# One decoder block on one core: attention steps in pairs, with the scores of four tiles in a row and one copy for two tiles

## The chip, the cores and the metric

The kernel runs on one core of one Trainium2 chip. The metric is the device time of one execution in microseconds (us). Of the engines, TensorE (PE in the profile; its weight loads are PEld), VectorE (DVE), ScalarE (ACT) and GpSimd (POOL) compute, and SyncE (SP) issues transfers. Each takes its instructions in the order in which they are written, and one engine waits for another through semaphores.

## The reference

One layer of a decoder block on an input of 1024 tokens by 1024 channels in float32. Two gated feed-forward half-steps stand around a middle part, which merges an attention and a pooling branch:

```python
h = h + 0.5 * swiglu(rms_norm(h, ffn1_norm), w1, w3, w2)
u = rms_norm(h, mix_norm);  q, k, v, pz, gates = split(u @ w_in)
y_attn = dilated_mixture_attention(q, k, v) @ w_branch_attn
y_pool = multiscale_pool(pz, pool_w, pool_scale) @ w_branch_pool
h = h + (sigmoid(gA) * y_attn + sigmoid(gB) * y_pool) @ w_out
h = h + 0.5 * swiglu(rms_norm(h, ffn2_norm), w1', w3', w2')
return rms_norm(h, final_norm)
```

The attention has 12 heads of 64 channels in three groups of four. A group has a window and a dilation: (128, 1), (512, 4), (2048, 16). A query attends to the keys t, t-r, t-2r and so on back to the window. The outputs of the three groups are added with weights from their softmax denominators.

## The kernel before

All products are made in single-precision parts: each operand is split into a high part and the rest, and three products (high by high, high by low, low by high) are added up in PSUM. The feed-forward halves and the input projection come first and last; they fill most of the time and the change does not touch them.

The change is in the attention loop (from line 1815). Its unit is a tile: one pair of heads (`hp`, two of them), one group (`g`, three) and one block of 128 queries (`i`, eight), which makes 48 tiles, listed in `slots`. A step `q` of the loop, 24 in all, takes the tiles 2q and 2q+1. Four steps make one pair of heads of one group. The order of the groups is 0, 1, 2 for the first pair of heads and 1, 2, 0 for the second. A tile has one or two blocks of keys (`blocks`): two in group 0 but for its first tile, one and two by turns in group 1, one in group 2.

The work of a tile runs through four steps of the loop, each engine in a written order (`manual_schedule`):

- `scores` (L1556): 6 matmuls a tile, three products for each of the two heads. The two heads use the lower and the upper 64 rows of the array, and each head writes a PSUM bank of its own. Banks come from two sets of four: "mm" for scores and rows of factors, "acc" for transposes, values and branch products. One bank is 512 columns of float32.
- `masked` (L1574): VectorE adds the mask and takes the row minimum; ACT makes the exponents (`exponents`, L1583).
- one step later `trans_p` (L1603): transposes of the exponents, which ACT splits (`ehi`, L1615) and VectorE completes (`elo`, L1618).
- two steps later `values` (L1636): the products with the values, both tiles of the step in one "acc" bank. 
- three steps later `gather` (L1654): VectorE copies them to `own`, 64 partitions by 128 elements, two copies a tile. In group 0 the 128 targets are next to each other, in group 1 they are 4 elements apart, in group 2 they are 8 apart.

Two things are woven in. `fill` (L1706) is the product of the pooling branch, which needs nothing of the attention: each `next(fill)` is four matmuls of 512 columns, three of them make one bank, and `end_branches` (L1720) multiplies that bank by the gate on VectorE. In the steps 18 to 21 the factors of the first pair of heads are applied: `f.rows()` transposes the factors of one group into an "mm" bank (L1537, four transposes, tile `fa`), and `f.product()` multiplies the gathered values by them on VectorE (L1673), which gives the bank back. Steps 18 and 20 make two such products each, 19 and 21 one each.

Beside that, ACT and GpSimd split the queries and keys of the next group (`split_ring`, L1216 and L1217), and SyncE loads what comes next.

Of the kernel before, what the change touches and what calls it, by code (L numbers as in the profile page):

```python
# [16 lines left out]
P = 128  # L17
S = 1024
D = 1024
NT = S // P  # L20
# [5 lines left out]
HD = 64  # L26
SC = HD ** -0.5
GROUPS = 3
# [8 lines left out]
def tokens(g, i):  # L37

    if g == 0:
        return i * P, 1, (i - 1 if i > 0 else None)  # L40
    if g == 1:
        r, b = divmod(i, 2)
        return r + 4 * P * b, 4, (i - 1 if b else None)
    return i, 8, None
# [74 lines left out]
def three(hi_lo_l, hi_lo_r):  # L119

    lh, ll = hi_lo_l
    rh, rl = hi_lo_r
    return ((lh, rh), (lh, rl), (ll, rh))
# [3 lines left out]
def tile_block(  # L127
# [29 lines left out]
    ve, ac, gp, pe = nc.vector, nc.scalar, nc.gpsimd, nc.tensor  # L157
# [10 lines left out]
    def bank(tag, name):  # L168
        return psum.tile([P, HALF], F32, tag=tag, name=name)
# [1032 lines left out]
    ring = {}  # L1202

    def load_ring(u, tile):

        ring[u] = []
        for a in range(2):
            y, hi = tile(F32, f"qk{u}_{a}_in"), tile(F32R, f"qk{u}_{a}_hi")
            nc.sync.dma_start(y, qk_dram[u][a].rearrange("h d c -> (h d) c"))
            ring[u].append((hi, y.bitcast(F32R), y))  # L1210

    def split_ring(u, n):

        hi, lo, y = ring[u][n // 2]
        c = (LOWS, HIGHS)[n % 2]
        ac.activation(hi[:, c], y[:, c], AF.Copy)  # L1216
        gp.tensor_tensor(lo[:, c], y[:, c], hi[:, c].bitcast(F32), op=OP.subtract)  # L1217
# [24 lines left out]
    def load_branch(d):  # L1242
        w, gb = row_part(f"wab{d}"), row(f"gb{d}")
        nc.sync.dma_start(w.rearrange("p (q c) -> p q c", q=2).bitcast(F32), late_w[1 + d][:, :, 256:768])
        nc.sync.dma_start(gb, gate_dram[d][:, 1])
        pool_in[d] = (w.rearrange("p (q c) -> p q c", q=2), gb)
# [116 lines left out]
    with tc.manual_schedule():  # L1363
# [4 lines left out]
        for k in range(len(items) + 4):  # L1368
# [6 lines left out]
            if k < len(items):  # L1375
                q, m = items[k]
# [3 lines left out]
            if k - 1 in results:  # L1380
                q, m = items[k - 1]
# [88 lines left out]
    slots = [(hp, g, i) for hp in range(HPAIRS) for g in ((0, 1, 2), (1, 2, 0))[hp] for i in range(NT)]  # L1470
    N = len(slots)
# [68 lines left out]
    def blocks(g, i):  # L1540

        return 1 if tokens(g, i)[2] is None else 2

    T = {}

    def scores(s):
        hp, g, i = slots[s]
        u = hp * GROUPS + g
        n = blocks(g, i)
        ks = slice((i + 1 - n) * P, (i + 1) * P)  # L1550
        ps = [bank("mm", f"s{s}_{a}")[:, :n * P] for a in range(2)]
        (qhi, qlo, _), (khi, klo, _) = ring[u]
        for j, (l, r) in enumerate(three((qhi, qlo), (khi, klo))):
            for a in range(2):
                rows = slice(a * HD, (a + 1) * HD)
                pe.matmul(ps[a], l[rows, i * P:(i + 1) * P], r[rows, ks], start=(j == 0), stop=(j == 2))  # L1556
        T[s] = {"s": ps}

    def masked(s):
        hp, g, i = slots[s]  # L1560
# [27 lines left out]
    def pair(q):  # L1588

        ns = [2 * blocks(*slots[s][1:]) * P for s in (2 * q, 2 * q + 1)]  # L1590
        return ((2 * q, 0, ns[0]), (2 * q + 1, ns[0], ns[1])), sum(ns)
# [16 lines left out]
    def split_p(q):  # L1608

        tiles, n = pair(q)  # L1610
        hi = a2.tile([P, 2 * HALF], F32R, tag="ehi", name=f"ehi{q}")
        lo = a2.tile([P, 2 * HALF], F32R, tag="elo", name=f"elo{q}")
        todo = tp.pop(q)
        for p, c0, w in todo:
            ac.activation(hi[:, c0:c0 + w], p, AF.Copy)  # L1615
        yield
        for p, c0, w in todo:
            ve.tensor_tensor(lo[:, c0:c0 + w], p, hi[:, c0:c0 + w].bitcast(F32), op=OP.subtract)  # L1618
        for s, c0, w in tiles:
            T[s]["pt"] = tuple(t[:, c0:c0 + w].rearrange("p (a b c) -> p a b c", a=2, c=P) for t in (hi, lo))  # L1620
        yield

    def values(q):
        both = bank("acc", f"o{q}")
        for s in (2 * q, 2 * q + 1):
            hp, g, i = slots[s]
            d = T[s]
            n = blocks(g, i)

            p = both[:, s % 2 * 2 * P:(s % 2 + 1) * 2 * P].rearrange("p (a c) -> p a c", a=2)  # L1630
            pt = d.pop("pt")
            j, end = 0, 3 * n - 1
            for b in range(n):
                c = slice((i + 1 - n + b) * P, (i + 2 - n + b) * P)
                for l, r in three(tuple(v[:, c] for v in v_of[hp * GROUPS + g]), tuple(w[:, :, b, :] for w in pt)):
                    pe.matmul(p, l, r, start=(j == 0), stop=(j == end))  # L1636
                    j += 1
            d["o"] = p
            if i == NT - 1:
                del v_of[hp * GROUPS + g]  # L1640

    own = {}

    def gather(s):

        hp, g, i = slots[s]
        p = T.pop(s)["o"]
        t0, step, _ = tokens(g, i)
        cols = slice(t0, t0 + step * (P - 1) + 1, step)
        if i == 0:  # L1650
            own[hp, g] = sums_o.tile([P, S], F32, tag="o", bufs=HPAIRS * GROUPS, name=f"o{hp}_{g}")
        for a in range(2):
            r = slice(a * HD, (a + 1) * HD)
            ve.tensor_copy(own[hp, g][r, cols], p[r, a, :])  # L1654

    att_parts = {}

# [69 lines left out]
    def send():  # L1727
        while stores:
            nc.sync.dma_start(*stores.pop())

    def branches():
        for n in range(2 * KT):
            yield from branch(n)

    fill = branches()
# [45 lines left out]
    def advance(gen, n=1):  # L1781
        for _ in range(n):
            next(gen, None)
# [24 lines left out]
    with tc.manual_schedule():  # L1808
        load_ring(uses[1], ring_tile)
        load_branch(1)  # L1810
        factors = [make_factors(hp, eng) for hp, eng in enumerate((gp, ve))]
        combines = [[Combine(hp, half, adds, lower) for half in range(2)]
                    for hp, (adds, lower) in enumerate((((gp, gp), gp), ((gp, ve), ve)))]
        splits = {}
        for q in range(N // 2):
            send()
            u, i = divmod(q, NT // 2)
            if 0 < u < len(uses) - 1 and i == 0:
                load_ring(uses[u + 1], ring_tile)
            scores(2 * q)  # L1820
            scores(2 * q + 1)
            if q == 1:
                next(fill)
                next(fill)
            if q > 0:
                trans_p(q - 1)
                splits[q - 1] = split_p(q - 1)
            if q > 1:
                next(fill, None)
                if q % 4 != 3:  # L1830
                    next(fill, None)
            if q > 2:
                gather(2 * q - 6)
                gather(2 * q - 5)
            masked(2 * q)
            masked(2 * q + 1)

            j = q - N // 4 - 6
            fa = [combines[0][j // 2]] * (2 - j % 2) if 0 <= j < 4 else []
            for f in fa:  # L1840
                f.rows()
            if q > 1:
                values(q - 2)
            if q > 0:
                advance(splits[q - 1], 2)
            for n in ((), (0,) if u > 0 else (), (2, 1) if u > 0 else (0, 2), (3,) if u > 0 else (1, 3))[i]:
                if u + 1 < len(uses):
                    split_ring(uses[u + 1], n)
            for f in fa:
                f.product()  # L1850
            end_branches()
            exponents(2 * q)
            exponents(2 * q + 1)
            house(2 * q)
            house(2 * q + 1)
        send()
        right_b.close()
        load_ya(3)
        load_merge(0)
        load_merge(1)  # L1860
        open_w_o()
        q = N // 2
        trans_p(q - 1)
        splits[q - 1] = split_p(q - 1)
        advance(factors[1])
        next(fill, None)
        values(q - 2)
        gather(2 * q - 6)
        gather(2 * q - 5)
        advance(splits[q - 1], 2)  # L1870
        advance(factors[1], 2)
        next(fill, None)
        end_branches()
        values(q - 1)
        for s in range(2 * q - 4, 2 * q):
            gather(s)
        for n in range(8):
            combines[1][n // 4].step()
            if n != 3:
                next(fill, None)  # L1880
            end_branches()
            send()
            if n == 3:
                load_merge(2)
        for k in (3, 4):
            load_merge(k)
# [34 lines left out]
    ops, banks = {}, {}  # L1921
# [66 lines left out]
    with tc.manual_schedule():  # L1988
# [66 lines left out]
        r = [rows_first2(t) for t in range(2)]  # L2055
# [211 lines left out]
```

## Time and profile before

| | |
|---|---|
| median of 3 runs | 1908.06 us (1907.91 to 1908.44) |
| the profiled execution: device time | 1908.0 us |
| its span, first to last instruction | 1906.2 us |
| granted TensorE clock | 0.999 |
| PE busy over the span | 1895.5 us (99%) |
| DVE, ACT, POOL busy over the span | 1336.2, 760.1, 731.0 us |
| the attention loop and its end | about 1042 to 1159 us of the span |

The profile is one execution. A line of a timeline gives start, duration, engine, source line and operation, output and inputs, shapes and count; lines of one kind that follow each other are merged. Starts of matmuls are recorded, their ends are modelled, so what counts on TensorE is the distance from one start to the next. The chain of waits is followed back from the last instruction and gives what was on the path at each time.

### The profile page before, as it was taken

The numbers are of one execution on the slowest core, as the hardware profiler recorded it, in microseconds if no ns is written. First come the engines' busy times: TensorE is split into PE (matmuls) and PEld (weight loads), VectorE is DVE, ScalarE is ACT, GpSimd is POOL, SyncE is SP. The second block draws the span as 40 slices with busy tenths as digits, with TensorE's granted clock in tenths as the row PEclk, the third lists the DMA queues.
The fourth block names the chain that finished last, engine by engine and source line by source line (L and its number), as shares of the span: only waits on it lengthen the run. The fifth ranks groups of instructions, "written<-read, shape, count | busy, mean of one in ns | idle before, by whom it ended". The sixth has DMA issues, their size and how long they took to land.

```text
span 1906.2 us, 24938 instructions
## 1 busy us (share of the span) xinstructions
PE 1895.5 (99%) x8946; PEld 1578.0 (83%) x8946; DVE 1336.2 (70%) x2016; ACT 760.1 (40%) x1364; POOL 731.0 (38%) x549
## 2 busy tenths in 40 slices
PE   9999999999999999999999999999999999999998
PEld 8888888888888888888888888888888888888886
DVE  7776556557776776667875896887675556577777
ACT  6323333333344443334444772353333323333344
POOL 5333333331223355444544456553333333312132
PEclk9999999999999999999999999999999999999999
DMA  4155222336466627655667977733433223453564
GB/s 190 50 193 177 83 89 105 138 110 215 148 233 219 204 92 247 220 212 198 228 232 286 302 233 265 269 148 123 164 119 122 84 88 117 149 197 135 194 220 166
DMA packets 144940, 331.98 MB, mean 174 GB/s; under 512 B 19120, under 2 KB 39856, under 8 KB 143280
## 3 DMA queue, kind: packets, MB, share of 16 engines
q1 hardware_dynamic: 137280, 308.00, 46.2%
q10 hardware_dynamic: 7536, 22.39, 3.3%
q8 instruction: 70, 1.15, 0.2%
q14 instruction: 54, 0.44, 0.1%
HBM read 229.61 MB, written 100.73 MB: 173 GB/s over the span
## 4 chain that ended last, share of the span: by engine, by line
PE 95%; DVE 2%; issue 1%; ACT 1%; POOL 1%; DMA 0%; POOLq 0%; ACTq 0%; DVEq 0%
PE u_mixm L331 19%; PE d_f L757 18%; PE wo L1958 4%; PE yp L1706 2%; PE o L1636 1%; PE ya L1771 1%; PE s L1556 1%; PE u_f20a L331 1%; PE u_f21b L331 1%; PE u_f20b L331 1%; PE u_f12b L331 1%; PE u_f12a L331 1%; PE u_f21a L331 1%; PE u_f11a L331 1%; PE u_f11b L331 1%
## 5 line engine op out<-in xcount | busy, mean ns | idle before, releaser
L757 PE MATMUL d_f<-bhi_f,ahi_f 128*128 128x512 f32 x616 | 240.7, 391 | 0.0
L757 PE MATMUL d_f<-bhi_f,alo_f 128*128 128x512 f32 x616 | 240.1, 390 | 0.0
L757 PE MATMUL d_f<-blo_f,ahi_f 128*128 128x512 f32 x616 | 240.0, 390 | 0.0
L719 POOL TENSOR_TENSOR alo_f<-g_f,ahi_f 128x512 fp32r<-128x512 f32 x60 | 83.5, 1408 | 294.0 <-ACT ahi_f L715 294.0
L331 PE MATMUL u_mixm<-xhi_t_mix,wc_mixm 128*128 128x512 f32 x608 | 157.7, 391 | 0.1
L757 PEld LDWEIGHTS d_f<-bhi_f,ahi_f 128*128 128x128 f32 x616 | 115.8, 188 | 23.9 <-DVE xlo_b_mix L410 0.2
L757 PEld LDWEIGHTS d_f<-blo_f,ahi_f 128*128 128x128 f32 x616 | 115.8, 188 | 23.8
L757 PEld LDWEIGHTS d_f<-bhi_f,alo_f 128*128 128x128 f32 x616 | 115.7, 188 | 23.8
L331 PEld LDWEIGHTS u_mixm<-xhi_t_mix,wc_mixm 128*128 128x128 f32 x608 | 113.6, 188 | 23.5 <-DVE xlo_t_mix L410 0.3
L331 PE MATMUL u_mixm<-xhi_b_mix,wc_mixm 128*128 128x512 f32 x456 | 121.3, 393 | 0.1
L309 POOL TENSOR_TENSOR wc_mixm<-s_mixm,wc_mixm 128x512 fp32r<-128x512 f32 x52 | 73.1, 1407 | 99.1 <-ACT wc_mixm L304 89.9
L331 PEld LDWEIGHTS u_mixm<-xhi_b_mix,wc_mixm 128*128 128x128 f32 x456 | 84.7, 188 | 17.4 <-issue 0.5
L304 ACT ACTIVATE wc_mixm<-s_mixm 128x512 fp32r<-128x512 f32 x76 | 46.9, 628 | 119.1 <-DVE s_mixm L363 53.4
L715 ACT ACTIVATE ahi_f<-g_f 128x1024 fp32r<-128x1024 f32 x84 | 81.8, 974 | 2.6 <-DMA g_f<-gs_f 2.6
L331 PE MATMUL u_mixm<-xlo_t_mix,wc_mixm 128*128 128x512 f32 x304 | 81.4, 390 | 0.0
L309 POOL TENSOR_TENSOR wc_mixm<-raw,wc_mixm 128x512 fp32r<-128x512 f32 x40 | 62.0, 1555 | 41.6 <-ACT wc_mixm L304 31.5
L715 ACT ACTIVATE bhi_f<-s_f2w 128x512 fp32r<-128x512 f32 x55 | 32.7, 627 | 95.0 <-DVE s_f2w L735 87.4
L331 PEld LDWEIGHTS u_mixm<-xlo_t_mix,wc_mixm 128*128 128x128 f32 x304 | 57.1, 188 | 12.0
L715 ACT ACTIVATE bhi_f<-s_f1w 128x512 fp32r<-128x512 f32 x55 | 32.7, 629 | 83.4 <-DVE s_f1w L735 78.6
L719 DVE TENSOR_TENSOR alo_f<-g_f,ahi_f 128x1024 fp32r<-128x1024 f32 (+1 forms) x48 | 57.6, 1200 | 8.0 <-ACT ahi_f L715 8.0
L331 PE MATMUL u_mixm<-xlo_b_mix,wc_mixm 128*128 128x512 f32 x228 | 61.1, 390 | 0.0
L1958 PE MATMUL wo<-w_o,o_hi 128*128 128x512 f32 x224 | 60.2, 391 | 0.0
(1320 smaller groups left out, 4785.7 us busy)
## 6 DMA issues: line engine op xcount, KB each, us to landing
g_f<-gs_f SPq DMA_DIRECT2D x70, 512.0 KB
gs_f<-y_f SPq DMA_DIRECT2D x88, 256.0 KB
raw<-in_w2a_dram SPq DMA_DIRECT2D x35, 512.0 KB
raw<-in_w2b_dram SPq DMA_DIRECT2D x35, 512.0 KB
gs_f<-gb_f SPq DMA_DIRECT2D x46, 256.0 KB
raw<-in_w1a_dram SPq DMA_DIRECT2D x22, 512.0 KB
raw<-in_w3a_dram SPq DMA_DIRECT2D x22, 512.0 KB
raw<-in_w1b_dram SPq DMA_DIRECT2D x22, 512.0 KB
```

The lines of the kernel that those rows point to most:

```text
L304: ac.activation(w[:, 0], src, AF.Copy)
L309: eng.tensor_tensor(w[:, 1], src, w[:, 0].bitcast(F32), op=OP.subtract)
L331: pe.matmul(p, a, b, start=(start and i == 0), stop=(i == 11), skip_group_check=not start)
L715: ac.activation(hi[:, c], src, AF.Copy)
L719: eng.tensor_tensor(lo[:, d], src[:, o], hi[:, d].bitcast(F32), op=OP.subtract)
L757: pe.matmul(self.banks[m][t], l, r, start=(first and q == 0), stop=(last and q == 2))
L1556: pe.matmul(ps[a], l[rows, i * P:(i + 1) * P], r[rows, ks], start=(j == 0), stop=(j == 2))
L1636: pe.matmul(p, l, r, start=(j == 0), stop=(j == end))
L1706: pe.matmul(p, a, b, start=(j == 0), stop=(j == 11))
L1771: pe.matmul(p, a, b, start=(j == 0), stop=(j == 5))
L1958: pe.matmul(banks[m][t], l, r, start=(st == 0 and n == 0), stop=(st == 1 and n == 5))
```

## The change

The loop's steps become long and short by turns.

- A long step (even q) makes the scores of its own two tiles and of the two tiles of the next step, 24 matmuls in a row. A short step (odd q) makes none. The two tiles of a step now share two banks, one for each head, in place of two banks for each tile.
- In a long step the values (of step q-2) come directly behind the transposes, ahead of `fill`. In a short step the order stays: transposes, `fill`, rows of factors, values.
- `gather` takes both tiles of a step at once: one copy of 64 partitions by 256 elements for each head. It is called in long steps alone, twice: for step q-3 ahead of the masks, and for step q-2 behind the low part of the split.
- From step 2 on `fill` is called three, one, two and one times in four steps, where it was two, one, two and two; the total is the same. In the long steps with a third call (q = 2, 6, 10 and so on), that call comes behind the second `gather`.
- In long steps the rows of factors come last on TensorE; in short steps they stay ahead of the values.

```diff
-    def scores(s):
+    def scores(q):
...
-        ps = [bank("mm", f"s{s}_{a}")[:, :n * P] for a in range(2)]
...
+        banks = [bank("mm", f"s{q}_{a}") for a in range(2)]
+        for s in (2 * q, 2 * q + 1):
...
+            c0 = s % 2 * 2 * P
+            ps = [b[:, c0:c0 + n * P] for b in banks]
...
-    def gather(s):
+    def gather(q):
...
-        cols = slice(t0, t0 + step * (P - 1) + 1, step)
...
         for a in range(2):
-            r = slice(a * HD, (a + 1) * HD)
-            ve.tensor_copy(own[hp, g][r, cols], p[r, a, :])
+            rows = own[hp, g][a * HD:(a + 1) * HD]
+            if g == 2:
+                to = rows.rearrange("p (c i) -> p i c", i=NT)[:, i:i + 2, :]
+            else:
+                to = rows[:, t0:t0 + step * (2 * P - 1) + 1:step].rearrange("p (s c) -> p s c", s=2)
+            ve.tensor_copy(to, both[a * HD:(a + 1) * HD, :, a, :])
...
-            scores(2 * q)
-            scores(2 * q + 1)
+
+            even = q % 2 == 0
+            if even:
+                scores(q)
+                scores(q + 1)
             if q == 1:
                 next(fill)
                 next(fill)
             if q > 0:
                 trans_p(q - 1)
                 splits[q - 1] = split_p(q - 1)
+            if even and q > 1:
+                values(q - 2)
             if q > 1:
                 next(fill, None)
-                if q % 4 != 3:
+                if even:
                     next(fill, None)
-            if q > 2:
-                gather(2 * q - 6)
-                gather(2 * q - 5)
+
+            if even and q > 2:
+                gather(q - 3)
             masked(2 * q)
             masked(2 * q + 1)
 
             j = q - N // 4 - 6
             fa = [combines[0][j // 2]] * (2 - j % 2) if 0 <= j < 4 else []
-            for f in fa:
-                f.rows()
-            if q > 1:
-                values(q - 2)
+            if not even:
+                for f in fa:
+                    f.rows()
+                if q > 1:
+                    values(q - 2)
             if q > 0:
                 advance(splits[q - 1], 2)
+            if even and q > 1:
+                gather(q - 2)
+            if q % 4 == 2 and q < N // 2 - 2:
+                next(fill, None)
+            if even:
+                for f in fa:
+                    f.rows()
...
-        gather(2 * q - 6)
-        gather(2 * q - 5)
+        gather(q - 3)
...
-        for s in range(2 * q - 4, 2 * q):
-            gather(s)
+        gather(q - 2)
+        gather(q - 1)
```

More of the change, by code (lines that the diff above doesn't have):

```diff
@@ L1544, in tile_block @@
     T = {}
-    def scores(s):
[L1547 to L1550, printed above, removed]
-        ps = [bank("mm", f"s{s}_{a}")[:, :n * P] for a in range(2)]
[L1552 to L1557, printed above, removed]
+    def scores(q):
+        banks = [bank("mm", f"s{q}_{a}") for a in range(2)]
+        for s in (2 * q, 2 * q + 1):
+            hp, g, i = slots[s]
+            u = hp * GROUPS + g
+            n = blocks(g, i)
+            ks = slice((i + 1 - n) * P, (i + 1) * P)
+            c0 = s % 2 * 2 * P
+            ps = [b[:, c0:c0 + n * P] for b in banks]
+            (qhi, qlo, _), (khi, klo, _) = ring[u]
+            for j, (l, r) in enumerate(three((qhi, qlo), (khi, klo))):
+                for a in range(2):
+                    rows = slice(a * HD, (a + 1) * HD)
+                    pe.matmul(ps[a], l[rows, i * P:(i + 1) * P], r[rows, ks], start=(j == 0), stop=(j == 2))
+            T[s] = {"s": ps}
     def masked(s):
@@ L1637, in values @@
                     j += 1
-            d["o"] = p
+            d["o"] = both
             if i == NT - 1:
@@ L1642, in tile_block @@
     own = {}
-    def gather(s):
-        hp, g, i = slots[s]
-        p = T.pop(s)["o"]
-        t0, step, _ = tokens(g, i)
-        cols = slice(t0, t0 + step * (P - 1) + 1, step)
+    def gather(q):
+        hp, g, i = slots[2 * q]
+        both = T.pop(2 * q)["o"].rearrange("p (s a c) -> p s a c", s=2, a=2)
+        del T[2 * q + 1]
         if i == 0:
             own[hp, g] = sums_o.tile([P, S], F32, tag="o", bufs=HPAIRS * GROUPS, name=f"o{hp}_{g}")
+        t0, step, _ = tokens(g, i)
         for a in range(2):
-            r = slice(a * HD, (a + 1) * HD)
-            ve.tensor_copy(own[hp, g][r, cols], p[r, a, :])
+            rows = own[hp, g][a * HD:(a + 1) * HD]
[4 more added lines that the diff above has]
+            ve.tensor_copy(to, both[a * HD:(a + 1) * HD, :, a, :])
     att_parts = {}
```

## The prediction

> **What bounds the kernel now.** I read the page first, then the stretch of the attention loop by engine, then the chain of waits inside it, then the starts of single matmuls.
>
> ```profile
> PE 1895.5 (99%) x8946; PEld 1578.0 (83%) x8946; DVE 1336.2 (70%) x2016; ACT 760.1 (40%) x1364; POOL 731.0 (38%) x549
> ```
>
> ```profile
> core 0: us, PE busy (x) PEld busy (x) DVE busy (x) ACT busy (x) POOL busy (x), PEclk, DMA share, GB/s
> 1042.00:1160.00 118.00, 117.35 (x884) 100.82 (x884) 104.37 (x370) 81.50 (x265) 49.63 (x44) 1.00 0.80 261
> 1111.00:1145.00 34.00, 34.00 (x264) 29.65 (x263) 32.32 (x112) 23.37 (x82) 19.40 (x20) 1.00 0.67 202
> ```
>
> TensorE bounds the loop, but VectorE is close behind: 104.4 of 118 us, and 32.3 of 34 where the factors are applied. Only what shortens TensorE's row counts, and only while VectorE can still follow. The chain runs on TensorE nearly throughout:
>
> ```profile
> 1048.16 1.97 ACT e L1583 x8
> ...
> 1053.53 0.91 PE s L1556 x12
> 1054.43 1.02 PE tp L1603 x8
> ...
> 1056.39 1.43 PE o L1636 x12
> ...
> 1073.41 0.80 PE tp L1603 x6
> ...
> 1080.75 0.82 PE s L1556 x12
> 1081.57 0.59 PE tp L1603 x4
> 1082.15 1.84 PE yp L1706 x8
> ...
> 1088.31 0.71 PE o L1636 x6
> ...
> 1125.85 1.01 PE s L1556 x12
> ...
> 1130.89 1.18 PE s L1556 x12
> ...
> 1151.02 0.44 PE fa L1537 x4
> ```
>
> Four transposes behind scores take 0.59; four of the same form behind a fill (fa) take 0.44. So scores cost something beyond their products. The starts show where:
>
> ```profile
> 1080.47 0.28 PE L1636 MATMUL o<-ehi,v_in 128*128 128x256 f32 x1
> 1080.68 0.33 PE L1556 MATMUL s<-qk_hi,qk_hi 64*128 64x128 f32 x2
> 1080.84 0.28 PE L1556 MATMUL s<-qk_in,qk_hi 64*128 64x128 f32 x2
> 1080.95 0.27 PE L1556 MATMUL s<-qk_hi,qk_in 64*128 64x128 f32 x2
> 1081.07 0.28 PE L1556 MATMUL s<-qk_hi,qk_hi 64*128 64x128 f32 x2
> ...
> 1081.29 0.28 PE L1556 MATMUL s<-qk_hi,qk_in 64*128 64x128 f32 x2
> 1081.49 0.33 PE L1603 MATMUL tp<-ident,e 128*128 128x128 f32 x1
> ```
>
> **Part 1: twelve runs of scores fewer.** Value products are 0.12 apart (1.43 for 12); the last one to the first scores is 0.21, so 0.09 is lost going in. The first pair takes 0.16 where the next take 0.11: 0.05. Going out, the transposes lose 0.59 - 0.44 = 0.15. That is 0.29 a run. The second tile of the run, in other banks, starts 0.12 behind (1080.95 to 1081.07): it pays nothing, so a third and a fourth should not either. With two key blocks the first pair loses 0.10, which makes 0.34:
>
> ```profile
> 1053.46 0.39 PE L1556 MATMUL s<-qk_hi,qk_hi 64*128 64x256 f32 x2
> 1053.68 0.28 PE L1556 MATMUL s<-qk_in,qk_hi 64*128 64x256 f32 x2
> ```
>
> The runs of twelve short steps go. Eight begin with one key block, four (q = 1, 3, 21, 23) with two: 8 x 0.29 + 4 x 0.34 = 3.7 us off TensorE. No run shows a tile with one key block behind one with two; the four joined runs of group 1 have this seam. I bound it between a gain of 0.05 and a loss of 0.05 each, and take nothing (0.2 in all).
>
> **Part 2: the start.** Transposes wait for exponents there:
>
> ```profile
> 1048.70 1.92 PE L1603 MATMUL tp<-ident,e 128*128 128x128 f32 x8 [0.26 <-ACT e L1583]
> ```
>
> They take 1.92 where 1.02 is usual, after 0.26 idle: 1.16 us of waiting. The scores of step 3 now stand ahead of them (0.91 by the row of 1053.53) and fit into that wait. 0.34 of it is counted above; the other 0.57 is gained too. Parts 1 and 2 make 4.3.
>
> **Part 3: ACT still keeps up.** The exponents of a long step must be ready for the transposes of the short one.
>
> ```profile
> 1055.12 1.09 ACT L1615 ACTIVATE ehi<-tp 128x512 fp32r<-128x512 f32 x2 [0.86 <-PE tp L1603]
> 1087.00 1.14 ACT L1216 ACTIVATE qk_hi<-qk_in 128x512 fp32r<-128x512 f32 x2
> ```
>
> With two key blocks everywhere, ACT needs 1.09 + 1.14 + 1.97 = 4.2 after the transposes; TensorE has 1.43 of values and three fills of 0.92 (half of 1.84), also 4.2, and the first half of the transposes needs only half the exponents, so about 1 us is spare. Where the third fill is missing, the splits of queries and keys are missing too. In a short step ACT needs 1.09 + 0.57 + 1.97 = 3.6 and TensorE has 0.92 + 1.43 + 1.7 of scores = 4.0. I cost this at nothing; without the third fill it would be some 0.9 a time. The first mask now waits for both tiles of its bank, 0.4 later; VectorE is then still at the copies of step q-3, which cover it. Values ahead of the fills are covered by the run of scores. Loads and stores are the same in number, only queued by longer and shorter steps on SP; the queues of GpSimd and SP keep their order.
>
> **Part 4: the copies.** A pair of tiles costs four copies now:
>
> ```profile
> 1063.03 1.20 DVE L1654 COPY o<-o 64x128 f32<-64x128 f32 x4 [0.96 <-PE o L1636]
> 1080.79 1.58 DVE L1654 COPY o<-o 64x128 f32<-64x128 f32 x4 [0.47 <-PE o L1636]
> ```
>
> ```profile
> L1618 DVE TENSOR_TENSOR elo<-tp,ehi 128x512 fp32r<-128x512 f32 x30 | 20.1, 684 | 0.6 <-ACT ehi L1615 0.6
> L1618 DVE TENSOR_TENSOR elo<-tp,ehi 128x256 fp32r<-128x256 f32 x10 | 4.2, 420 | 2.0 <-ACT ehi L1615 2.0
> ```
>
> That is 0.30 a copy to neighbouring targets and 0.40 to spread ones. 256 more elements cost 0.264, so 128 more cost 0.13. A copy of 256 neighbours comes to 0.43, an estimate. For spread targets the extra 0.10 may be paid once (0.40 + 0.13 = 0.53) or for each element (0.30 + 0.13 + 0.20 = 0.63); the dearest is 0.79, no saving at all. I take 0.63, since strides of 4 and of 8 cost alike and the extra then belongs to leaving the neighbour. The Trainium skill's page "Advanced Engine Details and Errata", section "Memory Cachelines", says that an access to SBUF that goes to another 16-byte line each time pays a penalty; by that rule too the extra is paid per element, and against the 0.53 the saving of this change shrinks by 0.2 for two copies. At 0.63 a pair saves 0.32, 24 pairs near 8 us of VectorE. None of it is on the path except between the steps 18 and 22.
>
> **Part 5: a new wait in steps 20 and 22.** A long step takes all four "mm" banks. Until step 21 rows of factors borrow them too, and VectorE gives a bank back with the product. Step 20's last bank is the one that step 19's rows borrowed. Behind that wait on TensorE stand the transposes, values and fills of the long step, and for them everyone.
>
> ```profile
> 1078.45 0.29 DVE L1574 CUSTOM_DVE_ANT_0 e<-s,mask 128x128 f32<-128x128 f32 x1
> ...
> 1079.30 1.02 DVE L1618 TENSOR_TENSOR elo<-tp,ehi 128x256 fp32r<-128x256 f32 x2
> ...
> 1118.02 0.25 DVE L1517 RECIPROCAL top<-top 128x16 f32<-128x16 f32 x1 [0.92 <-POOL top L1516]
> ...
> 1132.98 0.42 DVE L1574 CUSTOM_DVE_ANT_0 e<-s,mask 128x256 f32<-128x256 f32 x1
> ...
> 1134.36 1.01 DVE L1618 TENSOR_TENSOR elo<-tp,ehi 128x256 fp32r<-128x256 f32 x2
> 1135.30 0.68 DVE L1673 TENSOR_TENSOR o<-o,fa 128x512 f32<-128x512 f32 x1
> 1135.89 0.68 DVE L1720 TENSOR_TENSOR gb<-yp,gb 128x512 f32<-128x512 f32 x1
> ```
>
> When step 18's rows of factors end on TensorE, VectorE still has to make two products (0.59 each), the gate product and a low part (0.6 each, same length as the product), four masks (0.85, from 1078.45 to 1079.30) and step 19's product: 3.8, with about 0.4 of passing on between engines (a copy starts 0.32 behind the last value product: 1080.47, 1080.79). TensorE needs for step 19 0.44 + 0.92 + 0.44 + 0.71 and 0.8 of scores to come to that bank: 3.3. It waits 0.9. In step 22 the masks have two key blocks (1.38, from 1132.98 to 1134.36) and the low part is 0.94 long: 5.1 against 0.65 + 0.92 + 0.44 + 0.71 + 0.9 = 3.6, so 1.5. Of today's waits for such banks 0.19 (1.01 against 0.82) and 0.27 (1.18 against 0.91) go, about 0.5. VectorE's 0.92 of waiting for GpSimd ahead of step 18 grows behind a shorter step 17; I add 0.1. That makes +2.0.
>
> **The sum.** -4.3 + 2.0 = -2.3 on the profiled execution's 1908.0, which is 1.8 above its span and 0.06 below the median: 1905.7. About 0.2%, or 3.8 us, is what a measurement of this kernel can tell from no change, so this counts as none: 1904.2 and 1911.9 are the edges.
>
> **The rivals.** Faster: VectorE is far enough ahead that the banks are back in time; then today's 0.5 goes without a successor, 1908.0 - 4.3 - 0.5 = 1903.2. For it speaks the 8 us saved; against it that the chain of part 5 starts from TensorE's own end of the long step, whatever was saved before. 12 in 100.
>
> No gain: spread copies cost 0.79. Five pairs near the waits then take 0.32 more each, and nearly all of it, 1.5, lands on them: 1907.2. 12 in 100.
>
> The runs do not join: a seam between tiles of different steps costs half of what the switch did, 1.8: 1907.5. The rows of 1080.95 and 1081.07 speak against it. 5 in 100.
>
> Slower: the "acc" banks. A long step holds one or two for transposes, one for the values of q-2, one for those of q-3 until they are copied, and needs one for the fill: five of four where the transposes take two, in seven long steps (q = 2, 4, 6, 8, 14, 16, 22). If the fill gets the bank of the copied values, it is free 1.6 us into the step and nothing waits. If it gets one of the transposes, it waits for the low part: 1.26 of copies, 1.38 of masks, 1.2 of low part and 0.4, some 4.2, against 1.7 + 0.66 + 1.07 = 3.4; with VectorE a little late I price it at 1.0 a step: +7, 1912.7. It decides once VectorE enters the long steps over 2 us late, or by the choice of bank. 15 in 100.
>
> **How the numbers follow.** The forecast has 56 in 100. 0.53 for spread copies would take 0.6 off (0.2 less for each of three pairs ahead of the waits): 1905.1, the seam's bounds 0.2 either way. The range from 1903.0 to 1909.0 takes in all but the slower rival. Faster 0.15: the first rival and a little of the forecast's edge; slower 0.15; the rest is no change that can be told.
>
> **What would show it.** In the changed profile: 12 runs of 24 scores, and transposes of 0.44 in short steps; a copy of 64x256 near 0.43 and 0.63 (the records a little less); TensorE's starts with a gap of 1 to 1.5 inside the scores of steps 20 and 22, released by the products or the masks; no wait of fills in other long steps. Waits of the transposes for exponents beyond the start, or gaps ahead of the fills, would prove me wrong.

## The result and the profile after

The changed kernel takes 1905.01 us (median of 22 runs, 1904.38 to 1906.22); the kernel before took 1907.93 us beside it (22 runs). The ratio is 0.9985, with a 95% interval of 0.9979 to 0.9991. The forecast was 1905.7 us, no change that could be told; 2.9 us less came out. The interval leaves out 1, so 22 runs of each kernel do tell this change, where the prediction took 0.2% for the least that can be told.

The page of the changed kernel, its line of busy times:

```profile
PE 1891.6 (99%) x8946; PEld 1574.5 (83%) x8946; DVE 1329.1 (70%) x1968; ACT 760.1 (40%) x1364; POOL 731.3 (38%) x549
```

TensorE has 3.9 us less, its weight loads (PEld) 3.5, and VectorE 7.1 us less in 48 instructions fewer; ScalarE and GpSimd stayed. The change sits between the first product of scores and the first product of the output projection (`ya`), so I measure it there. The rows of the timelines, first of the kernel before, then of the changed one:

```profile
1041.95 0.33 PE L1556 MATMUL s<-qk_hi,qk_hi 64*128 64x128 f32 x2
...
1159.07 4.25 PE L1771 MATMUL ya<-att,ya 128*128 128x512 f32 x18
```

```profile
1041.59 0.33 PE L1560 MATMUL s<-qk_hi,qk_hi 64*128 64x128 f32 x2
...
1156.44 6.75 PE L1779 MATMUL ya<-att,ya 128*128 128x512 f32 x29
```

From start to start that is 117.12 us before and 114.85 after: **the loop is 2.27 us shorter, where -2.3 was forecast.** The rest of the 2.9 lies outside. In the two profiled executions 0.36 us of it lie ahead of the loop and 0.1 behind. The work behind the loop is the same in all kernels below, and yet the time from `ya` to the end differs among their profiled executions from 746.7 to 748.4 us; why, no run here shows. I therefore give the loop beside the median and argue from the loop.

The chain of waits of the changed kernel, from the load that step 11 waits for to step 17, shows the runs:

```profile
1075.04 10.79 DMA qk_in<-qk
...
1087.01 1.55 ACT e L1587 x8
...
1088.61 0.33 PE tp L1607
1088.94 0.94 PE yp L1714 x4
...
1090.58 1.57 PE s L1560 x24
1092.15 0.59 PE tp L1607 x4
1092.74 0.71 PE o L1640 x6
...
1106.61 1.49 PE s L1560 x24
...
1111.82 0.44 PE tp L1607 x4
1112.26 0.93 PE yp L1714 x4
```

24 scores in a row take 1.49 (one key block) and 1.57 (one and two), where two runs of 12 took 0.82 and some 0.9 each. Four transposes take 0.59 behind scores and 0.44 in the short step by the rows of the chain, as foretold; from their first start to the next product's it is 0.41 and 0.36. Values follow the transposes, and fills the values, without a gap.

The timeline of the changed kernel at the steps 11, 20 and 22 shows what was paid:

```profile
1087.63 1.31 PE L1607 MATMUL tp<-ident,e 128*128 128x128 f32 x4
1088.69 0.48 PE L1714 MATMUL yp<-xlo_b_mix,wab 128*128 128x512 f32 x1
...
1123.11 0.76 PE L1560 MATMUL s<-qk_hi,qk_hi 64*128 64x128 f32 x2
1123.64 0.34 PE L1560 MATMUL s<-qk_in,qk_hi 64*128 64x128 f32 x2
...
1124.95 0.38 PE L1560 MATMUL s<-qk_hi,qk_hi 64*128 64x256 f32 x1 [0.38 <-DVE o L1681]
...
1125.85 0.66 PE L1607 MATMUL tp<-ident,e 128*128 128x128 f32 x4
...
1132.69 0.51 PE L1560 MATMUL s<-qk_hi,qk_hi 64*128 64x256 f32 x2
...
1134.68 0.38 PE L1560 MATMUL s<-qk_hi,qk_hi 64*128 64x256 f32 x1 [0.89 <-DVE o L1681]
...
1135.58 1.09 PE L1607 MATMUL tp<-ident,e 128*128 128x128 f32 x8
```

The scores of step 20 take 1123.11 to 1125.85, 2.74 us. The same run takes 1.60 in two kernels below where it does not wait, so 1.14 is waiting. (Its first tile has one key block and the other three have two.) Those of step 22 take 2.89, 1.26 over the 1.63 that they take without a wait (all two key blocks). Both stop at a product with factors (`o`, L1681), as forecast; step 20 stops ahead of that for a mask of step 19 (0.43 between its first two starts). The four transposes of step 11 take 1.06 to the next start where 0.36 is usual: 0.70 that nobody forecast.

### The profile page after: what moved, and what is told of

Its sections match the earlier page's. It is cut to its first block, busy times and chain, and to the rows that moved or that the text cites. A ratio compares the mean times of both kernels' runs of the same rounds, so it can differ in the third digit from the quotient of the medians.

```text
span 1903.4 us, 24895 instructions
## 1 busy us (share of the span) xinstructions
PE 1891.6 (99%) x8946; PEld 1574.5 (83%) x8946; DVE 1329.1 (70%) x1968; ACT 760.1 (40%) x1364; POOL 731.3 (38%) x549
## 4 chain that ended last, share of the span: by engine, by line
PE 96%; DVE 1%; DMA 1%; ACT 1%; issue 0%; POOL 0%; SPq 0%; POOLq 0%; ACTq 0%
PE d_f L757 22%; PE u_mixm L331 19%; PE wo L1978 4%; PE yp L1714 2%; PE ya L1779 1%; PE u_f20a L331 1%; PE u_f12b L331 1%; PE u_f12a L331 1%; PE u_f11a L331 1%; PE u_f20b L331 1%; PE u_f21b L331 1%; PE u_f11b L331 1%; PE u_f21a L331 1%; PE u_f210b L331 1%; PE u_f210a L331 1%; PE u_f29b L331 1%
```

## The experiments

Each time is a median over 9 to 11 runs (22 for the first two rows); the kernel before, beside them, stayed at 1907.9 to 1908.1. The loop comes from one profiled execution. Its stretches without a wait agree between the kernels within 0.03 us, but the wait in step 11 alone lies between 0.13 and 0.70 in the kernels that load as the changed one does, so a difference of some tenths can be that.

| kernel | median, us | loop, us |
|---|---|---|
| before | 1907.9 | 117.12 |
| changed | 1905.0 | 114.85 |
| before + joined scores | 1907.1 | 116.36 |
| before + joined copies | 1906.7 | 116.18 |
| before + shared banks of scores | 1907.6 | 116.75 |
| before + load earlier | 1908.3 | 117.26 |
| changed, steps 0 to 3 apart | 1906.6 | 115.77 |
| changed, values behind the fills | 1911.1 | 119.99 |
| changed, four copies | 1905.8 | 114.90 |
| changed, rows in other banks | 1906.2 | 114.67 |
| changed, factors later | 1905.4 | 114.46 |
| changed, product first | 1904.5 | 113.78 |
| changed, load earlier | 1903.6 | 113.09 |
| changed, load earlier and product first | 1903.4 | 112.34 |

**The parts by themselves.** First the scores alone, on the kernel before. The two tiles of a step share their banks here too, as in the changed kernel:

```diff
-            scores(2 * q)
-            scores(2 * q + 1)
+            if q % 2 == 0:
+                scores(q)
+                scores(q + 1)
```

> The kernel before, with the scores of four tiles in a row in every long step and nothing else: the four copies for a pair, the order of values and fills, and the number of fills in each step stay as they were. Theory (the joined scores need the rest of the change, since a long step takes all four banks of scores and a short step must be long enough for ACT): the 12 runs of scores go as in the changed kernel (-3.7 and -0.6 at the start), but waits of TensorE for banks, exponents and splits give most of it back; -0.4 us against the kernel before, between -1.5 and +1.5, and the trace shows those waits in many long steps. Rival (the order and the copies are beside the point, the waits are those of steps 20 and 22 alone): -4.3 + 2.0 to 2.5, so -1.8 to -2.3 us, at most 1 us behind the changed kernel.

The loop lost 0.76 us: inside the theory's range, and the rival is out. The saving of the runs is there (24 scores in 1.49 to 1.57 again), but transposes wait for exponents in the steps 3, 7, 11 and 15 (0.35 to 0.6 each), the scores of step 20 wait 0.8 for banks, and in step 21 0.5 is lost behind the fill and 0.4 behind the rows. The waits for exponents stand in short steps, where the theory had looked for them in long ones.

Then the copies alone: `gather(q - 3)` with the two copies of the changed kernel, where four copies stood.

> The kernel before, with one copy for two tiles in the place where the four copies of a pair stood, and nothing else. Theory A (VectorE ends only the two waits for banks inside the scores of steps 20 and 22, 0.19 and 0.27 us, and the wait of the start is not its own): 48 copies less and some 7 us of VectorE freed, and the time falls by at most 0.5 us. Theory B (VectorE's length between the steps 18 and 23 comes back on TensorE wherever factors are applied): about -1.0 us, with the scores of those steps at 0.8 to 0.9 without gaps. Both expect copies of 64x256 near 0.42 for neighbours and 0.62 for spread targets.

The loop lost 0.94, the size of theory B. The two waits of the kernel before at such banks went nearly whole (its scores of step 20 take 1.01 where 0.89 is usual there, those of step 21 1.18 where 0.91 is). That is 0.36, and 0.1 more went in step 19. The largest part, 0.44, lies behind the last step: the transposes, the fill and the values there take 0.91, 1.25 and 1.51 in the kernel before and 0.79, 1.01 and 1.43 here. The copies of VectorE and the first product of those values, in the kernel before and then here:

```profile
1145.67 1.19 DVE L1654 COPY o<-o 64x128 f32<-64x128 f32 x4
...
1147.00 0.35 PE L1636 MATMUL o<-ehi,v_in 128*128 128x256 f32 x1
```

```profile
1144.37 0.86 DVE L1658 COPY o<-o 64x256 f32<-64x256 f32 x2
...
1145.97 0.28 PE L1636 MATMUL o<-ehi,v_in 128*128 128x256 f32 x1
```

In the kernel before the product comes 0.14 behind the end of the four copies, here 0.74 behind the end of the two. That the values wait there for the bank that the copies give back is read from these rows; the profile names no releaser. The price of a copy was as expected (below). The two parts by themselves give 0.76 + 0.94 = 1.7 of the 2.27, each without the order of the changed kernel.

**The order of the values.** The changed kernel, with the values of the long step behind its fills:

```diff
-            if even and q > 1:
-                values(q - 2)
             if q > 1:
                 next(fill, None)
                 if even:
                     next(fill, None)
+            if even and q > 1:
+                values(q - 2)
```

> The changed kernel, with the values of the long steps behind the two fills (where they stood before the change) and nothing else. Theory (ACT and VectorE get the second and third bank of a long step back late when copies and low parts come later; the place of the values keeps them ahead): 2 to 5 us slower than the changed kernel, with waits of transposes and values for banks or exponents in several long steps. Rival (only the joining matters): within 0.3 us of the changed kernel.

The loop grew by 5.14 us and the median by 6.1: the theory, just past its upper end. This one line of order is worth more than the whole change. Its waits in the loop:

```profile
DVE o L1662 <- PE o L1640: 13.9, 11, 1.7
...
PEld tp L1607 <- ACT e L1587: 3.6, 13, 0.5
...
PE tp L1607 <- DVE o L1662: 1.5, 2, 1.2
PEld tp L1607 <- ACT ehi L1619: 1.4, 1, 1.4
```

VectorE now stands 13.9 us before copies, since the values it copies come last in the long step (1.2 us in the changed kernel). Behind the copies stand its masks, and behind those ACT's exponents: the transposes wait 3.6 for them (1.9 in the changed kernel), and 1.5 for a bank that a copy gives back. The last is the mechanism of the slower rival, banks of the set "acc" that return late. It was real, and the place of the values is what kept it out.

**The start.** The changed kernel, with the steps 0 to 3 making their own scores (`if q < 4: scores(q)`, then pairs as before):

> The changed kernel, with the scores of the steps 0 to 3 made each in its own step; from step 4 on two steps in a row as before this edit. Theory (two runs of 0.34 come back, and the wait for the first exponents is not filled by the scores of step 3): 2 x 0.34 + 0.57 = 1.25 us slower than the changed kernel. Rival (the start gains nothing but the two runs): 0.7 us slower. Third (the wait at the start is only moved, and the long step 2 pays later): no difference.

0.92 us more in the loop, between theory and rival. (The first four steps by themselves take 1.04 more, from 15.21 to 16.25 us; 0.12 came back later, 0.05 of it in step 11.) The theory had a miscount in it. It took back two runs, but the steps 0 and 1 stand together in every kernel, since nothing lies between them; only step 3's run came back. 0.34 + 0.57 = 0.91 is what is left of the sum, against the 0.92 of the loop and the 1.04 on the spot. So what did the change bring in the steps 0 and 1, whose scores take 2.78 us before (1041.95 to 1044.73) and 1.76 after? That was asked of the kernel before, with two banks a step instead of four:

```diff
-            scores(2 * q)
-            scores(2 * q + 1)
+            scores(q)
```

> The kernel before, where the two tiles of a step share two banks of scores as in the changed kernel (four banks before), each step making its own scores, and nothing else of the change. Theory (in the kernel before the scores of the steps 0 and 1 stand together already, 24 products in 2.78 us, and wait for banks that masks give back; with two banks a step they fit into the four and take 1.76 us, as in the changed kernel, and the waits of 0.19 and 0.27 us in the steps 21 and 22 go too): the loop shortens by 1.0 at the start and by up to 0.5 at the waits, 1.0 to 1.5 us in all. Rival (sharing makes the first mask of a pair wait for both tiles, and exponents come later by as much): the first scores take 1.76 us but the transposes behind them wait longer, and the loop stays within 0.3 us.

The scores did take 1.76 us, 1.02 less. But their exponents were not ready that much sooner, and the transposes of step 1 took back 0.6. The timeline of this kernel, from step 1's transposes on:

```profile
1045.12 1.42 PE L1607 MATMUL tp<-ident,e 128*128 128x128 f32 x6
...
1047.71 1.91 PE L1607 MATMUL tp<-ident,e 128*128 128x128 f32 x8 [0.27 <-ACT e L1587]
```

The six transposes took 0.82 in the kernel before. 0.4 is left at the start. The two old waits, in the steps 20 and 21, went too (0.39), but as much came back at values that wait for low parts and at rows, so the whole loop lost 0.37; neither theory nor rival had the number. A wait ahead of another wait is worth only their difference.

**The waits of the steps 20 and 22.** First the bank itself: the rows of factors of the short steps 19 and 21 in "acc" banks (`f.rows("acc")`), so that no long step waits for them.

> The changed kernel, with the rows of factors of the short steps 19 and 21 in banks of the other kind (those of transposes, fills and values) and not in those of the scores. Theory A (VectorE is the bound in this stretch and the bank is only where TensorE meets it): the gaps inside the scores of steps 20 and 22 shrink to what the masks end, and as much comes back as waits of fills, values or rows for their banks in steps 19 to 22; 0.0 to 0.6 us slower than the changed kernel. Theory B (the bank itself is the cost): 1.5 to 1.9 us faster, and no new wait.

The scores of both steps ran in 1.60 and 1.63, without a gap. The loop stayed, 0.18 shorter, and that only because step 11 happened to wait 0.13 and not 0.70 in this execution; without this it would be some 0.4 longer. (The median is 1.1 longer; in the profiled execution that lies behind the loop, which takes the 748.4 us there.) The waits turned up elsewhere. The waits of this kernel in the loop:

```profile
PEld o L1640 <- DVE elo L1622: 1.3, 1, 1.3
PEld fa L1537 <- DVE gb L1728: 1.1, 1, 1.1
...
PEld o L1640 <- DVE gb L1728: 0.7, 1, 0.7
```

Theory A: VectorE is the bound here, and the bank is only where TensorE meets it.

Then VectorE's chain: the product of the steps 19 and 21 ahead of the low part.

```diff
                 for f in fa:
                     f.rows()
+                    f.product()
...
-            for f in fa:
-                f.product()
+            if even:
+                for f in fa:
+                    f.product()
```

> The changed kernel, with the product of the steps 19 and 21 ahead of the low part of the exponents in VectorE's order (it stood behind it). Theory (the bank that the long steps 20 and 22 wait for comes back with this product, and VectorE's chain up to it is what counts): the low part, 0.6 us in step 19 and 0.94 us in step 21, leaves that chain; of the gaps inside the scores the part that the product ends goes (0.65 us in step 20, 0.9 of 1.17 us in step 22), the part that the masks end stays; 1.2 to 1.5 us faster than the changed kernel. Rival (the gap only moves, since the delayed low parts are late for the values or their banks): no difference, the gaps turn up at the transposes or values of steps 20 to 23.

The scores of step 20 fell from 2.74 to 2.15 and those of step 22 from 2.89 to 1.97: 1.5 gone, as the theory says. 0.4 came back between the transposes and the values of step 22 and 0.2 at the transposes behind step 23, so the loop lost 1.07 and the median 0.5. The part of the gaps that the masks end stayed.

What VectorE does before was tried in two ways. With four copies for a pair again, in the places of the two:

> The changed kernel with four copies of 64x128 for two tiles again, in the places where the two copies of 64x256 stand. VectorE gets some 7 us more to do. Theory A (the waits inside the scores of steps 20 and 22 start from TensorE's own long step, so what VectorE does ahead of it does not move them, and elsewhere VectorE is ahead): the gaps in steps 20 and 22 stay within 0.2 us, and the time grows by 0.0 to 0.5 us against the changed kernel. Theory B (with the old copies VectorE has no room in the steps 17 to 23): 1.2 to 2.0 us slower, with new waits of transposes, rows and values for VectorE there.

The loop did not move (0.05), but this does not decide between the theories: VectorE hardly got more to do. The group of the copies in this kernel:

```profile
L1663 DVE COPY o<-o 64x128 f32<-64x128 f32 x96 | 27.9, 357 | 1.7 <-PE o L1640 1.2
```

It covers 27.9 us, against 26.9 for the 48 joined copies. In the kernel before 96 copies of the same mean, 357 ns, cover 34.3. What this means stands at the end. What the saved time of the copies is worth inside the changed kernel stays open.

And with the reciprocal of the factors behind the copies of step 18:

```diff
-        if N // 2 + 8 <= s < N // 2 + 11:
+        if N // 2 + 8 <= s < N // 2 + 10:
             advance(factors[0])
...
                 gather(q - 3)
+            if q == N // 4 + 6:
+                advance(factors[0])
```

> The changed kernel, with the last piece of the factors (GpSimd's sums, VectorE's reciprocal, GpSimd's rows) behind the copies of step 18 in the order of the engines and not at the end of step 17. VectorE then copies while GpSimd still sums, and does not stand 2.0 us before the reciprocal. Theory (the gap of step 20 that the product ends, 0.65 us, comes from these 2.0 us, which moving the load removed in part): VectorE's wait falls under 1.0 us, that gap goes, step 22 keeps its 1.2 us and step 11 its 0.65 us; 0.5 to 0.7 us faster than the changed kernel. Rival (the load alone did it, by the DMA): no difference.

VectorE's wait fell from 2.0 to 0.9 and the scores of step 20 from 2.74 to 2.02. But 0.3 came back at the transposes of step 21 and 0.5 at its values, which now waited for the gate product (`gb`). The loop lost 0.39, of which 0.3 is again a shorter wait in step 11 (0.37 for 0.70). The theory's gain failed: the wait only moved, and the median stayed within 0.4.

**The load.** In the changed kernel the transposes of step 11 wait for exponents, since ACT has waited for queries and keys. Its view of waits has a line that the kernel before does not have in the loop:

```profile
ACT qk_hi L1216 <- DMA qk_in<-qk: 1.8, 2, 0.9
```

SyncE's queue, first before, then after:

```profile
1068.23 0.94 SPq L1435 DMA_DIRECT2D w_o_in<-in_w_o_dram  x2
1076.96 0.34 SPq L1729 DMA_DIRECT2D by_pool<-gb  x1
1077.39 1.20 SPq L1209 DMA_DIRECT2D qk_in<-qk  x2
```

```profile
1072.69 0.32 SPq L1737 DMA_DIRECT2D by_pool<-gb  x1
1073.06 1.31 SPq L1435 DMA_DIRECT2D w_o_in<-in_w_o_dram  x2
1074.47 0.94 SPq L1209 DMA_DIRECT2D qk_in<-qk  x2
```

With the third fill of the steps 2 and 6, the twelfth fill falls in step 6 and not in step 7. So the store of its result (`by_pool`), sent at the start of the next step, stands ahead of the load of the output projection's factors (`w_o_in`), started at the end of step 7, and no longer behind it. SyncE waits for that store, and the load then goes out right ahead of the queries and keys. These go out earlier than in the kernel before (1074.47 against 1077.39), but ACT gets to them some 2 us earlier as well, and by the chain above 10.79 us pass until they are there. The edit starts the load of `w_o_in` two calls earlier:

```diff
-        if N - 34 <= s < N - 13:
+        if N - 36 <= s < N - 15:
             advance(first)
```

> The changed kernel, with the load of the output projection's factors started two calls of the loop earlier (so that it stands ahead of a store and of the loads of queries and keys in SP's queue, and not right between them). Theory (in the changed kernel this load goes directly ahead of the loads of queries and keys, ACT waits 0.9 us twice for those, and the transposes of step 11 wait 0.65 us for exponents): ACT's waits for these loads shrink under 0.3 us, the transposes start 0.11 apart, and the time falls by 0.6 to 0.8 us against the changed kernel. Rival (the wait at these transposes has another cause, ACT's splits themselves): no difference, and the gap stays.

The four transposes of step 11 take 0.60 by their row instead of 1.31, and ACT does not wait there. But the loop lost 1.76 us and the median 1.4, twice the expectation. The other half is in the steps 20 (2.03 for 2.74) and 22 (2.70 for 2.89). GpSimd's timelines, changed kernel and then this one, show where it came from:

```profile
1111.90 0.29 POOL L1510 TENSOR_TENSOR w<-top,stats 128x48 f32<-128x48 f32 x1 [3.53 <-DVE top L1509]
1112.14 2.56 POOL L1452 TENSOR_TENSOR w_o<-w_o_in,w_o 128x512 fp32r<-128x512 f32 x2
...
1116.56 0.22 POOL L1516 TENSOR_TENSOR top<-top,f 128x16 f32<-128x16 f32 x1
```

```profile
1107.17 2.54 POOL L1452 TENSOR_TENSOR w_o<-w_o_in,w_o 128x512 fp32r<-128x512 f32 x2 [0.99 <-ACT w_o L1451]
1110.93 0.29 POOL L1510 TENSOR_TENSOR w<-top,stats 128x48 f32<-128x48 f32 x1 [1.23 <-PE yp L1714]
...
1114.49 0.22 POOL L1516 TENSOR_TENSOR top<-top,f 128x16 f32<-128x16 f32 x1
```

The split of this load, 2.56 us on GpSimd, stood between two operations of the factors, and VectorE waited behind it for 2.0; now it is done before, and VectorE waits 1.4. That both halves belong to the load is shown by the one edit; that the second comes by GpSimd is read from these rows, not tried alone. On the kernel before the same edit does nothing:

> The kernel before, with the load of the output projection's factors started two calls earlier, as in the run of that name on the changed kernel. Theory (the load was harmless in the order of before: its transposes show no wait at that place, and the gaps of the steps 20 and 22 are 0.1 to 0.3 us): the loop shortens by 0.0 to 0.3 us. Rival (the load was always in the way, and the 1.4 us are a gain that has nothing to do with the change): the loop shortens by 1.0 us or more.

The loop did not shorten but grew by 0.14, all of it at the transposes of step 12 (0.55 for 0.41). The theory had looked for a gain of up to 0.3; the rival with its 1.0 is out. The load only costs in the order of the changed kernel.

**Both.** The load earlier and the product first:

> The changed kernel, with the load started two calls earlier and the product of the steps 19 and 21 ahead of the low part. If the waits are separate, the loop loses the 1.76 us of the first and, of the 1.07 us of the second, the part of step 22 (0.9 us), since step 20's wait is largely gone already: loop 112.2 us, time near 1902.7 us. If they are one wait seen at two places, the loop stays at 113.1 us.

The loop is 112.34 us, as the sum of separate waits had it (112.2), and the scores of the steps 20 and 22 take 1.60 and 1.82. The median is 1903.38 us (1902.65 to 1904.88), a ratio to the kernel before of 0.9976 (0.9967 to 0.9985). It beats both kernels; against the load alone, 1903.62, only the loop tells it apart.

## Why the prediction was right

The main costs, the runs that go and the new waits in the steps 20 and 22, came out as forecast and for the reasons forecast. That the loop came out within 0.1 us of the forecast is luck: smaller errors cancelled.

- **Part 1, the runs.** The price was right. Two runs of one key block, 0.82 each, became 1.49: 0.15, and the transposes of short steps take the 0.44 as read. The seam between one and two key blocks gains 0.05, the better end of its bounds (1.57 against 0.88 + 0.89 by the starts). The count was wrong: 11 runs went, not 12, since the steps 0 and 1 stood together. 0.34 too much.
- **Part 2, the start.** The scores of step 3 in the wait for exponents: 0.91 forecast with their run, 1.04 on the spot when undone. Overlooked was that two tiles now share banks, which brings 0.4 at the start and made up for the run that did not exist.
- **Part 3.** Priced at nothing, it cost 0.70, and by the prediction's own sign (waits of transposes for exponents beyond the start) this part was wrong. The step that failed is "the queues of GpSimd and SP keep their order": the third fill moved a store past a load in SyncE's order, the queries and keys came late to ACT, and step 11 paid for it. It is also the least steady term, 0.13 to 0.70 over the kernels that load as this one does. Elsewhere ACT keeps up, and no fill of a long step waited.
- **Part 4, the copies.** From start to start 0.42 to 0.43 for neighbours and 0.57 to 0.69 for spread targets, against 0.43 and 0.63; the cheap end of 0.53 is out, and so is 0.79. Two pairs of the changed kernel's timeline, of group 0 and of group 2:

```profile
1065.77 0.86 DVE L1662 COPY o<-o 64x256 f32<-64x256 f32 x2 [0.42 <-PE o L1640]
...
1094.02 1.33 DVE L1662 COPY o<-o 64x256 f32<-64x256 f32 x2
```

- The size was right and its reason only in part. By the Trainium skill's page "Advanced Engine Details and Errata", section "Memory Cachelines", an access that goes to a new 16-byte line each time is slower. The 0.6 to 0.7 against 0.43 agree with that. But the four copies of the experiment took 1.33 with the same spread targets where the kernel before took 1.62, so the lines are not all of it.
- **Part 5, the banks.** The mechanism, the places and the sum were right: 1.14 + 1.26 = 2.40 against 0.9 + 1.5. That the sum fits so well is chance, since one wait was longer and the other shorter than forecast. In step 20 VectorE's wait for GpSimd grew from 0.92 to 2.02, where I had added 0.1. With that wait at 0.9 again, in the kernel with factors later, step 20 waits only 0.42: by that run the 0.9 forecast for it was too much by half, and the longer wait made it up. Of the waits before, 0.39 went (0.5 forecast): the 0.19 of step 20 was measured against 0.82, the length of scores with one key block, but its tiles have one and two, whose scores take 0.89, so that wait was 0.12.

Put together from start to start, with a fill that moved ahead of step 4 counted at 0.92:

| steps | change, us | of it |
|---|---|---|
| 0 to 3 | -1.50 | step 3 -1.04, the start -0.4, under 0.1 in other places |
| 4 to 19 | -1.73 | eight runs (0.30 with one key block, else 0.35) -2.6; step 11 +0.70, step 13 +0.17 |
| 20 to the end | +0.96 | two runs -0.7, old waits -0.39, behind the last step -0.45; new waits +2.40, rows of factors +0.1 |

The sum is the measured -2.27. The 0.45 behind the last step stands in no part of the prediction, which looked for no gain from shorter copies there; the joined copies alone brought the same 0.44.

Of the rivals, "the banks are back in time" fell with the gaps of the steps 20 and 22, "the runs do not join" with the 1.49. A copy at 0.79 fell with the 0.57 to 0.69. Of the "acc" banks 0.17 is left in this kernel, at the transposes of step 13, which need two of them. The load of the weights of the third transpose:

```profile
1095.47 0.42 PEld L1607 LDWEIGHTS tp<-ident,e 128*128 128x128 f32 x4 [0.19 <-issue]
```

It comes 0.12 behind the end of the copies of 1094.02 shown above (1.33 long), and 0.11 to 0.12 behind it in the seven other kernels with the values ahead of the fills, so I read it as the bank that these copies give back; the profile names no releaser, and it was not tried alone. With the values behind the fills such waits grow.

That the forecast counted the new place of the values at nothing, as covered, was right as a price and hid that it is the part on which the rest depends.

## What to carry to other kernels

Count what a reordering moves past what on every queue, those of the transfers too: here a fill that ended one place earlier put a store ahead of a load, and one moved line gave 1.4 us. A gap inside one engine's work belongs to the chain that ends it; giving TensorE other banks moved the wait, taking one operation out of VectorE's chain gained 1.07 us of the loop. And a step that looks free because it is covered may be the cover of everything behind it: move it alone before calling it free.

## What the runs showed of the hardware

Copies of VectorE from 64 partitions to the same 64 partitions follow each other faster than copies that alternate between the lower and the upper half. The same four copies of 64x128 for a pair, with spread targets, in the kernel before (lower, upper, lower, upper):

```profile
1096.16 1.62 DVE L1654 COPY o<-o 64x128 f32<-64x128 f32 x4
```

and in the changed kernel with four copies (lower, lower, upper, upper):

```profile
1097.88 1.33 DVE L1663 COPY o<-o 64x128 f32<-64x128 f32 x4
```

By the single starts, a spread copy in this order begins 0.22 to 0.26 us behind the one ahead of it when both are in the same half (once 0.17), and 0.39 to 0.46 when the half changes; the alternating order takes 0.39 to 0.43 each (once 0.34). To neighbouring targets it is 0.20 to 0.21 and 0.28 to 0.29, against 0.28 to 0.31 each. Single copies are as long in both kernels (357 ns in the mean), so in the same half the next begins before the last has ended, and after a change of half only when it has. Two copies of 64x128 that stay in their half take about as long as one copy of 64x256 to spread targets. By the groups above, 96 copies in the new order and places cover 6.4 us less, where joining them saved 7.4. Why the change of half costs this, no run here shows.
